# Hybrid encoder layer: output projection in token blocks, two of them projected ahead of FFN2's operands

## Chip, cores and metric

The kernel runs on one core of a Trainium2 chip. The metric is the device time of one execution in microseconds (us), as the median of several runs. TensorE is called PE here, VectorE DVE, ScalarE ACT, GpSimd POOL and SyncE SP, as in the profile.

## What is computed

One layer of an encoder on 1024 tokens of a new stream and 64 tokens of a running one, 1088 in all, with a model width of 1024 and FFN width of 2816. Cut to what matters here:

```python
def modulate(x, gain, shift, scale):
    return rms_norm(x, gain) * (1 + scale[:, None, :]) + shift[:, None, :]

def swiglu_ffn(h, w_up, w_down):
    gate, up = jnp.split(h @ w_up, 2, axis=-1)
    return (jax.nn.silu(gate) * up) @ w_down
...
    mixed = jnp.concatenate(
        [sb_o.reshape(B, T, SB_WIDTH).astype(x.dtype),
         jax.nn.silu(r_g) * head_group_norm(ret_o).reshape(B, T, RET_WIDTH).astype(x.dtype)],
        axis=-1) @ w_out
    x = x + g2[:, None, :] * mixed

    h = modulate(x, norm_ffn2, sh3, sc3)
    x = x + MACARON_WEIGHT * g3[:, None, :] * swiglu_ffn(h, ffn2_w_up, ffn2_w_down)
```

`sb_o` comes from stick-breaking attention, `ret_o` from a retention of four heads. Before this stands a first FFN of the same form.

## The kernel before

**Data.** Features lie on the partitions and tokens on the free axis. The residual stream is in eight tiles `A[0]` to `A[7]` of 128 x 1088. An fp32 product is made of three matmuls (`mm3`, L197 to L199): each operand is split into a high part, cast on ACT (L225 for data, L81 for weights), and a low part, subtracted on DVE or POOL (L226, L86); then high x high, low weight x high, and high weight x low are added in one PSUM bank. `H[k]` and `L[k]` hold the high and low part of an operand. Weights come in units of 1024 columns (`Units`): `load` starts the DMA of two halves of 128 x 512, `split` makes their two parts, `done` frees them. Tokens are cut into three chunks (384, 384, 320), or into four blocks of `BL` = 272.

**Output projection.** After the mix, `take` splits the eight concatenated head tiles into `H`, `L`. The last one (`lastk` = 7) is ready only when the last retention head is done. So `out_units` first adds up the seven `early` k for each of the eight output tiles d (one weight unit per d) and each chunk, 21 matmuls a group (tile `wo`), and is woven by estimated costs (`weave`) with the matmuls of that last head, `retain(3)`. The residual add (`resid`, L243) reads the bank and adds it to `A[d]`. Then a loop over the blocks 0, 2, 1, 3 makes the product with the last k alone, 3 matmuls for each d (tile `wl`), adds it to `A[d]`, stores `A[d]` for later (`xs`), and squares it for FFN2's norm (`Norm`): `square` on ACT with sums on POOL and DVE, `fold` on PE (tile `st`), `factors` on DVE and POOL (tile `rx`), and `rows` on PE (tile `rb`), which spreads the factors of a block over the partitions.

**FFN2's operands.** The up projection uses seven products instead of eight on 2 x 2 blocks (`ORDER`): the width is cut into k and k + 4, the tokens into blocks b and b + 2. Half s = 0 of each product takes blocks 0 and 2, half s = 1 blocks 1 and 3. For every k of 0 to 3 and every s, `x_build` multiplies four pieces of `A` by the norm's rows (L404, DVE), scales them on ACT (L407), forms t1 to t4 by differences (L412) and splits all seven operands (b11, t1, t2, b21, t3, t4, b22). In the kernel before, POOL takes the difference t3 and four of the seven splits, DVE the rest. The s = 0 builds are due at set times during the last two blocks of the output projection, the s = 1 builds beside up tile 0.

**Up tiles.** `Up.prep(f)` loads four weight halves of tile f, forms four sums (L466, DVE) and splits seven weights. `product(f, p, s)` is 12 matmuls of 272 columns, `read` takes the result from PSUM (L518, L521, L524, L528). A tile has 7 products x 2 halves x 12 = 168 matmuls. Tile 0 is written out by hand: the first three products by k as the operands come, for s = 0, and the same for s = 1; all others come product by product (`Up.tile`), with the conditioning's products beside tiles 1 to 18.

**What sets the order.** The program's order and the scheduler's own model set the order on each engine, and DVE keeps the program's order from tile 1 on. Each engine then works strictly through its own list.

## Time and profile before

| | |
|---|---|
| median of 3 runs | 2315.87 us (2313.78 to 2322.09) |
| the profiled execution | 2316.76 us, its span 2314.7 us |
| PE busy | 2184.9 us, 94% |
| DVE busy | 1505.9 us, 65% |
| POOL busy | 1051.6 us, 45% |
| ACT busy | 832.8 us, 36% |
| mean granted clock of PE | 0.971 |

Busy shares are means over the whole span. Two engines can each be far from full and yet bound a stage in turn, so the stage is read by windows and by waits. A matmul's listed duration is longer than the distance from one to the next, since they are pipelined; what a row of them costs is taken from their starts.

### The profile page before, as it was taken

Reading aid. Unit: us, or ns where it says so; the run is one execution under the profiler, and the core shown is the slowest. Engines: PE = TensorE matmul, PEld = TensorE weight load, DVE = VectorE, ACT = ScalarE, POOL = GpSimd, SP = SyncE. Lnnn points to the kernel's source line nnn. Section 1 sums busy time; section 2 is a strip of 40 time slices with the busy share of each in tenths; the row PEclk is TensorE's granted clock in tenths of the full one; section 3 lists DMA queues with packets and bytes.
Section 4 is the critical chain, followed back from the end, with each engine's and each line's share of the span. In section 5 each row is a group of like instructions: output and inputs, shape, how many; then the busy total and the mean of one; then the engine's idle time right before and its main releaser. Section 6 shows DMA issues by size and latency. Waiting matters only on the chain. (4 is left out here: it accounts for less than half of the span.)

```text
span 2314.7 us, 40167 instructions
## 1 busy us (share of the span) xinstructions
PE 2184.9 (94%) x15188; PEld 2140.0 (92%) x15188; DVE 1505.9 (65%) x2902; ACT 832.8 (36%) x1724; POOL 1051.6 (45%) x1004
## 2 busy tenths in 40 slices
PE   5899999999999988888989999968999999999999
PEld 4799999999999988888889998957999999999999
DVE  5767777755777878887773555386555555556666
ACT  5522322232221346655663333155332323322221
POOL 3444444453444565434443444266444444544442
PEclk8899999999999999999999999977999999999999
DMA  7233333336343321011001012122222222352322
GB/s 247 92 122 128 112 129 112 130 108 225 124 128 118 123 64 55 22 41 38 27 30 67 32 40 108 44 90 71 90 93 87 91 85 84 104 181 83 101 82 102
DMA packets 116609, 220.35 MB, mean 95 GB/s; under 512 B 14528, under 2 KB 55488, under 8 KB 116416
## 3 DMA queue, kind: packets, MB, share of 16 engines
q1 hardware_dynamic: 116416, 217.79, 27.9%
q8 instruction: 120, 1.97, 0.4%
q14 instruction: 73, 0.60, 0.1%
HBM read 174.88 MB, written 42.86 MB: 94 GB/s over the span
## 5 line engine op out<-in xcount | busy, mean ns | idle before, releaser
L243 DVE SCALAR_TENSOR_TENSOR A<-dn,mod,A 128x384 f32<-128x384 f32 (+1 forms) x704 | 329.6, 496 | 148.5 <-PE dn L199 147.6
L197 PE MATMUL dn<-hs,wh 128*128 128x384 f32 (+1 forms) x1056 | 348.7, 330 | 3.4 <-DVE A L243 3.4
L199 PE MATMUL dn<-hl,wh 128*128 128x384 f32 (+1 forms) x1056 | 348.1, 330 | 0.0
L198 PE MATMUL dn<-hs,wl 128*128 128x384 f32 (+1 forms) x1056 | 348.1, 330 | 0.0
L86 POOL TENSOR_TENSOR wl<-wr,wh 128x512 fp32r<-128x512 f32 x162 | 220.3, 1366 | 142.5 <-ACT wh L81 140.3
L197 PE MATMUL pj<-Hh,wh 128*128 128x384 f32 (+1 forms) x672 | 235.5, 350 | 1.7 <-DVE A L243 1.7
L226 POOL TENSOR_TENSOR hl<-hr,hs 128x384 fp32r<-128x384 f32 x132 | 131.3, 1011 | 228.9 <-ACT hs L225 227.0
L199 PE MATMUL pj<-Lh,wh 128*128 128x384 f32 (+1 forms) x672 | 222.9, 332 | 0.0
L198 PE MATMUL pj<-Hh,wl 128*128 128x384 f32 (+1 forms) x672 | 221.5, 330 | 0.0
L197 PEld LDWEIGHTS dn<-hs,wh 128*128 128x128 f32 x1056 | 199.1, 189 | 3.8 <-DVE A L243 3.7
L198 PEld LDWEIGHTS dn<-hs,wl 128*128 128x128 f32 x1056 | 199.1, 189 | 0.0
L199 PEld LDWEIGHTS dn<-hl,wh 128*128 128x128 f32 x1056 | 199.1, 189 | 0.0
L518 DVE TENSOR_TENSOR u<-p,p 128x272 f32<-128x272 f32 x176 | 77.3, 440 | 165.8 <-PE p L199 165.7
L225 ACT CAST hs<-hr 128x384 fp32r<-128x384 f32 x132 | 65.4, 496 | 323.2 <-PE dn L198 158.4
L197 PE MATMUL p<-xt,wh1s 128*128 128x272 f32 x528 | 154.2, 292 | 0.9 <-DVE u L518 0.9
L199 PE MATMUL p<-xt,wh1s 128*128 128x272 f32 x528 | 153.8, 291 | 0.7 <-DVE xt L226 0.7
L198 PE MATMUL p<-xt,wl1s 128*128 128x272 f32 x528 | 154.0, 292 | 0.0
L81 ACT CAST wh<-wr 128x512 fp32r<-128x512 f32 x162 | 98.1, 619 | 151.3 <-PE wo L199 50.8
L86 POOL TENSOR_TENSOR wl1a<-wr1a,wh1a 128x512 fp32r<-128x512 f32 x66 | 94.2, 1430 | 124.8 <-ACT wh1a L81 118.5
L86 POOL TENSOR_TENSOR wl2a<-wr2a,wh2a 128x512 fp32r<-128x512 f32 x66 | 87.5, 1326 | 102.1 <-ACT wh2a L81 102.0
L197 PEld LDWEIGHTS pj<-Hh,wh 128*128 128x128 f32 x672 | 127.9, 190 | 4.7 <-issue 2.7
L198 PEld LDWEIGHTS pj<-Hh,wl 128*128 128x128 f32 x672 | 128.0, 190 | 0.3
(324 smaller groups left out, 6685.6 us busy)
## 6 DMA issues: line engine op xcount, KB each, us to landing
wa<-in_wada SPq DMA_DIRECT2D x56, 512.0 KB, 3.6
hd<-hh SPq DMA_DIRECT2D x44, 544.0 KB, 2.7
wr1a<-in_wup SPq DMA_DIRECT2D x88, 256.0 KB, 2.8
wr<-in_wdn SPq DMA_DIRECT2D x88, 256.0 KB, 2.9
wr2a<-in_wup SPq DMA_DIRECT2D x88, 256.0 KB, 2.8
hr<-hd SPq DMA_DIRECT2D x88, 192.0 KB, 2.5
wr<-in_win SPq DMA_DIRECT2D x56, 256.0 KB, 2.7
au<-in_wada SPq DMA_DIRECT2D x16, 512.0 KB, 5.7
```

What stands on the lines that cost most here:

```text
L81: self.nc.scalar.copy(h, raw)
L86: self.nc.gpsimd.tensor_tensor(l, raw, h.bitcast(F32), op=ALU.subtract)
L197: nc.tensor.matmul(ps[:, :w], wh, xh, start=first, stop=False, skip_group_check=read_between)
L198: nc.tensor.matmul(ps[:, :w], wl, xh, start=False, stop=False, skip_group_check=read_between)
L199: nc.tensor.matmul(ps[:, :w], wh, xl, start=False, stop=last, skip_group_check=read_between)
L225: nc.scalar.copy(hi, src)
L226: eng.tensor_tensor(lo, src, hi.bitcast(F32), op=ALU.subtract)
L243: nc.vector.scalar_tensor_tensor(A[d][:, s0:s0 + sw], ps[:, s0 - c0:s0 - c0 + sw], mod[:, s, b, d:d + 1], A[d][:, s0:s0 + sw], op0=ALU.mul ...
L518: nc.vector.tensor_tensor(new(name), ps[:, :BL], v[y, s], op=ALU.add)
```

## The change

The output projection goes by blocks instead of chunks. Its early part makes blocks 0 and 2 alone, for d = 0 to 6, beside the last retention head; d = 7 and the product with the last k follow for these two blocks. Then blocks 1 and 3 are projected in full, 24 matmuls a group (tile `wb`), d in the order of `PAIRS`; for this the eight weight units are loaded and split a second time. Beside it FFN2's operands of s = 0 are built (`build_first`), all differences and splits on DVE now; b22 of s = 0 is split after the blocks are done. The residuals of `A[0]` and `A[4]` for blocks 1 and 3 go to separate tiles `xb`. Then come the norm of blocks 1 and 3 and the operands of s = 1, and up tiles 0 and 1 by pairs of blocks: s = 0 of tile 0, s = 0 of tile 1, s = 1 of tile 1, s = 1 of tile 0, the weights of tile 0 being loaded and split again for the last. Tiles 2 to 21 go as before, the conditioning's products beside 2 to 19.

```diff
+    PAIRS = [0, 4, 1, 5, 2, 6, 3, 7]
     wu.add([I["wout"][u] for u in range(9)])
+    wu.add([I["wout"][u] for u in PAIRS])
...
+    def x_first(pool):
+
+
+        keys = [(name, part, k, 0) for k in range(4) for name in SETS[:6] for part in range(2)]
+        for i in range(4):
+            put(pool.tile([P, NTOK], F32R, name=f"xe{i}", bufs=1), keys[4 * i:4 * i + 4])
+        places = [t[k][:, cols(blk)] for k in range(KT) for t in (H, L) for blk in (0, 2)]
+        X.update(zip(keys[16:], places))
+
+    def x_second():
+
+        keys = [(name, part, k, 1) for k in range(4) for name in SETS for part in range(2)]
+        places = [t[k][:, cols(blk)] for k in range(KT) for t in (H, L) for blk in (1, 3)]
+        X.update(zip(keys, places))
+        return keys[32:]
+
+    def over_x(kt, keys):
+        A[kt] = xpool.tile([P, NTOK], F32R, tag=f"A{kt}", name=f"x1A{kt}")
+        put(A[kt], keys)
...
-        less("t3", "b22", "b12", nc.vector if whole else nc.gpsimd)
+        less("t3", "b22", "b12", nc.vector)
...
-        for i, name in enumerate(SETS):
-            split_h(b[name], X[name, 0, k, s], X[name, 1, k, s], nc.gpsimd if i % 2 == 0 else nc.vector)
+    def x_split(b, names, k, s):
+        for name in names:
+            split_h(b[name], X[name, 0, k, s], X[name, 1, k, s], nc.vector)
...
-        def out_units(ds):
-            for d in ds:
+        def take(k, blk, eng):
+            split_h(A[k][:, cols(blk)], H[k][:, cols(blk)], L[k][:, cols(blk)], eng)
+
+        def out_units(blks):
+
+            for d in range(lastk):
                 u = U_WOUT + d
                 wu.load(min(u + 3, U_WOUT + 8))
-                for c in range(3):
-                    yield from out_early(d, c)
-                    if c == 1:
+                for i, blk in enumerate(blks):
+                    p = pt("pj", f"wo{d}_{blk}")
+                    for j, k in enumerate(early):
+                        acc_cols(p, u, [k], blk * BL, BL, j == 0, j == len(early) - 1)
+                        if j % 2 == 1:
+                            tick()
+                            yield 6 * BL / 2.4
+                    resid(p, BSEGS[blk], d, 5)
+                    yield 3 * BL / 2.4
+                    if i == 0:
                         wu.split(u + 1)
                 wu.done(u)
...
         hl_tiles("m", early)
-        for c in range(3):
+        for i, blk in enumerate((0, 2, 1, 3)):
             for k in early:
-                take(k, c)
+                take(k, blk, nc.gpsimd if (k + i) % 3 == 0 else nc.vector)
         for k in early:
             nc.sync.dma_start(A[k], xs[k])
-        weave(out_units(range(lastk)), retain(3), 7 * 63 * 155.0 * 0.8, RROOM)
+        weave(out_units((0, 2)), retain(3), 7 * 42 * 125.0 * 0.8, RROOM)
         hl_tiles("m", [lastk])
-        for c in range(3):
-            take(lastk, c)
+        for blk in (0, 2, 1, 3):
+            take(lastk, blk, nc.vector)
         nc.sync.dma_start(A[lastk], xs[lastk])
-        drain(out_units([lastk]))
...
+    xb = {d: hnpool.tile([P, 2 * BL], F32, name=f"xb{d}", bufs=1) for d in (0, 4)}
+
+    def xv(d, blk):
+        if d in xb and blk % 2 == 1:
+            return xb[d][:, blk // 2 * BL:(blk // 2 + 1) * BL]
+        return A[d][:, cols(blk)]
...
+    def build_first(k):
+
+        b = later[k] = x_parts([(name, kt, blk * BL, xv(kt, blk), ns[blk].rb[:, :BL]) for name, kt, blk in
+                                (("b11", k, 0), ("b12", k, 2), ("b21", k + 4, 0), ("b22", k + 4, 2))],
+                               hnpool, 2, k, 0, False, ("b22",))
+        x_split(b, SETS[:6], k, 0)
+
+    def finish_x(po, d, blk):
+        resid(po, BSEGS[blk], d, 5, xv(d, blk))
+        nc.sync.dma_start(xs[d][:, cols(blk)], xv(d, blk))
+        ns[blk].square(d, xv(d, blk))
...
-    for i, blk in enumerate((0, 2, 1, 3)):
-        c0 = blk * BL
-        for d in range(KT):
-            po = pt_any(f"wl{blk}_{d}", ("wt", "z"))
-            mm3(po, BL, *wu.get(U_WOUT + 8, d), H[lastk][:, c0:c0 + BL], L[lastk][:, c0:c0 + BL], True, True)
-            resid(po, BSEGS[blk], d, 5)
-            nc.sync.dma_start(xs[d][:, c0:c0 + BL], A[d][:, c0:c0 + BL])
-            ns[blk].square(d)
+    wu.load(U_WOUT + 9)
+    for blk in (0, 2):
+        for d in [lastk] + early:
+            po = pt_any(f"wl{blk}_{d}", ("wt", "z")) if d != lastk else pt("pj", f"wl{blk}_{d}")
+            if d == lastk:
+                acc_cols(po, U_WOUT + d, early, blk * BL, BL, True, False)
+            mm3(po, BL, *wu.get(U_WOUT + 8, d), H[lastk][:, cols(blk)], L[lastk][:, cols(blk)], d != lastk, True)
+            finish_x(po, d, blk)
             due(6 * BL / 2.4)
+            if d == 3 and blk == 0:
+                wu.split(U_WOUT + 9)
         at(now[0] + 2000, ns[blk].fold)
         at(now[0] + 2000, ns[blk].factors)
-        if i < 2:
-            at(now[0] + 4000, ns[blk].rows, "av" if blk < 2 else "ms")
-        if i == 1:
-            for k in range(4):
-                at(now[0] + 4100 + 1500 * k, x_build, k, 0, 2, rb_of, hnpool)
-        next(weights, None)
+        at(now[0] + 4000, ns[blk].rows, "av" if blk == 0 else "ms")
+    wu.done(U_WOUT + 7)
+    wu.done(U_WOUT + 8)
+    for k in range(4):
+        at(now[0] + 4100 + 6500 * k, build_first, k)
+    weights = up.prep(0)
+    for i, d in enumerate(PAIRS):
+        u = U_WOUT + 9 + i
+        if i < KT - 1:
+            wu.load(u + 1)
+        for blk in (1, 3):
+            po = pt("pj", f"wb{d}_{blk}")
+            ks = early + [lastk]
+            for j in range(0, KT, 2):
+                acc_cols(po, u, ks[j:j + 2], blk * BL, BL, j == 0, j == KT - 2)
+                due(6 * BL / 2.4)
+            finish_x(po, d, blk)
+            if blk == 1 and i < KT - 1:
+                wu.split(u + 1)
+        wu.done(u)
+        if i >= KT - 2:
+            next(weights)
     drain(weights)
-    wu.done(U_WOUT + 8)
     due(1e6)
+    for blk in (1, 3):
+        ns[blk].fold()
+        ns[blk].factors()
+        ns[blk].rows("av" if blk == 1 else "ms")
+    for i, d in enumerate((0, 4)):
+        over_x(d, [("b22", part, k, 0) for k in (2 * i, 2 * i + 1) for part in range(2)])
+    for k in range(4):
+        x_split(later[k], ("b22",), k, 0)
+    rest = x_second()
...
+    for k in range(4):
+        b = x_parts([(name, kt, blk * BL, xv(kt, blk), ns[blk].rb[:, :BL]) for name, kt, blk in
+                     (("b11", k, 1), ("b12", k, 3), ("b21", k + 4, 1), ("b22", k + 4, 3))],
+                    hnpool, 2, k, 1, False)
+        if k > 0:
+            over_x(k, rest[8 * k - 8:8 * k - 4])
+            over_x(k + 4, rest[8 * k - 4:8 * k])
+        x_split(b, SETS, k, 1)
+    hnpool.release()
+
+    prep = up.prep(1)
+    for p in ORDER:
+        up.product(0, p, 0)
+        up.read(0, p, 0)
+        next(prep, None)
+    drain(prep)
+    for p in ORDER:
+        up.product(1, p, 0)
+        up.read(1, p, 0)
+    prep = up.prep(0)
+    for k in range(4):
+            up.product(1, p, 1, [k])
+    for p in ORDER[:3]:
+        up.read(1, p, 1)
+        next(prep, None)
+    for p in ORDER[3:]:
+        up.product(1, p, 1)
+        up.read(1, p, 1)
+        next(prep, None)
+    drain(prep)
+    prep = up.prep(2)
+    for p in ORDER:
+        up.product(0, p, 1)
+        up.read(0, p, 1)
+        next(prep, None)
+    drain(prep)
...
```

What moves on DVE while the last two blocks are projected. Names: `wl`, `wb` are PSUM tiles of a group, `hn2b` and `hn2t` pieces and differences, `x0H`, `xe`, `Hm`, `Lm` operands; the source line numbers of the changed kernel are a few higher. Before, among the residuals of block 3:

```order
L412 TENSOR_TENSOR hn2t_17502<-hn2b_17493,hn2b_17490 128x272
L243 SCALAR_TENSOR_TENSOR A_7_6457<-wl_7_17524,mod,A_7_6457 128x272
L412 TENSOR_TENSOR hn2t_17504<-hn2b_17499,hn2t_17502 128x272
L226 TENSOR_TENSOR x0H_17223<-hn2t_17502,x0H_17223 128x272
L412 TENSOR_TENSOR hn2t_17508<-hn2b_17496,hn2t_17504 128x272
L226 TENSOR_TENSOR x0L_17224<-hn2b_17496,x0L_17224 128x272
L243 SCALAR_TENSOR_TENSOR A_0_6450<-wl_0_17545,mod,A_0_6450 128x208
L226 TENSOR_TENSOR x0H_17225<-hn2t_17508,x0H_17225 128x272
L243 SCALAR_TENSOR_TENSOR A_0_6450<-wl_0_17545,mod,A_0_6450 128x64
```

After the change, the residual of unit 4, block 3, and the next one:

```order
L246 SCALAR_TENSOR_TENSOR xb_17003<-wb_3_17390,mod,A_4_6454 128x208
L424 TENSOR_TENSOR hn2t_17429<-hn2b_17424,hn2t_17427 128x272
L424 TENSOR_TENSOR hn2t_17431<-hn2b_17424,hn2b_17418 128x272
L424 TENSOR_TENSOR hn2t_17433<-hn2b_17421,hn2t_17429 128x272
L229 TENSOR_TENSOR xe_17007<-hn2b_17415,xe_17007 128x272
L229 TENSOR_TENSOR xe_17007<-hn2t_17427,xe_17007 128x272
L229 TENSOR_TENSOR Hm_16282<-hn2t_17429,Hm_16282 128x272
L229 TENSOR_TENSOR Lm_16283<-hn2b_17421,Lm_16283 128x272
L229 TENSOR_TENSOR Hm_16284<-hn2t_17431,Hm_16284 128x272
L229 TENSOR_TENSOR Lm_16285<-hn2t_17433,Lm_16285 128x272
L246 SCALAR_TENSOR_TENSOR xb_17003<-wb_3_17390,mod,A_4_6454 128x64
L246 SCALAR_TENSOR_TENSOR A_1_6451<-wb_1_17456,mod,A_1_6451 128x272
```

Before, one or two building operations stand between residuals. Now three differences and six splits of one k stand between the two parts of one residual.

What moves on DVE in the building of s = 1. Before, from k = 1 (`x1A`, `xe` operands of k = 0, `rb_1`, `rb_3` the norm's rows):

```order
L404 TENSOR_TENSOR hn2b_17871<-A_1_6451,rb_1_17821 128x272
L226 TENSOR_TENSOR x1A_17856<-hn2b_17840,x1A_17856 128x272
L404 TENSOR_TENSOR hn2b_17874<-A_1_6451,rb_3_17825 128x272
L226 TENSOR_TENSOR xe_17775<-hn2t_17853,xe_17775 128x272
L404 TENSOR_TENSOR hn2b_17878<-A_5_6455,rb_1_17821 128x272
L404 TENSOR_TENSOR hn2b_17881<-A_5_6455,rb_3_17825 128x272
```

After the change, the same place for k = 1:

```order
L229 TENSOR_TENSOR Lm_16289<-hn2b_18066,Lm_16289 128x272
L229 TENSOR_TENSOR Hm_16290<-hn2t_18080,Hm_16290 128x272
L229 TENSOR_TENSOR Lm_16291<-hn2t_18082,Lm_16291 128x272
L229 TENSOR_TENSOR Hm_16292<-hn2b_18073,Hm_16292 128x272
L229 TENSOR_TENSOR Lm_16293<-hn2t_18084,Lm_16293 128x272
L229 TENSOR_TENSOR Hm_16294<-hn2t_18086,Hm_16294 128x272
L229 TENSOR_TENSOR Lm_16295<-hn2b_18076,Lm_16295 128x272
L416 TENSOR_TENSOR hn2b_18104<-A_2_6452,rb_1_17997 128x272
```

Before, DVE splits three of seven operands, between the next k's products; now it splits all seven in a row, and the next k's products come behind them.

What moves on PE between the halves of the first tiles. `p_20_0` is tile 0, s = 0, and `p_21_1` tile 1, s = 1. Before:

```order
L199 MATMUL p_20_0_17790<-x0H_17233,wh2s_0_17754 128x272
L197 MATMUL p_20_0_17790<-x0L_17236,wh2s_0_17754 128x272
L198 MATMUL p_20_0_17790<-x0L_17236,wl2s_0_17756 128x272
L199 MATMUL p_20_0_17790<-x0L_17236,wh2s_0_17754 128x272
L197 MATMUL p_20_1_18048<-x1A_17855,wh2a_0_17407 128x272
L198 MATMUL p_20_1_18048<-x1A_17855,wl2a_0_17409 128x272
```

After the change:

```order
L201 MATMUL p_21_1_18432<-x1A_18126,wl2a_1_18219 128x272
L200 MATMUL p_21_1_18436<-x1A_18127,wh2s_1_18238 128x272
L201 MATMUL p_21_1_18436<-x1A_18127,wl2s_1_18240 128x272
L200 MATMUL p_21_1_18440<-x1A_18127,wh2s_1_18242 128x272
L201 MATMUL p_21_1_18440<-x1A_18127,wl2s_1_18244 128x272
L202 MATMUL p_21_1_18432<-x1A_18126,wh2a_1_18217 128x272
L202 MATMUL p_21_1_18440<-x1A_18127,wh2s_1_18242 128x272
L202 MATMUL p_21_1_18436<-x1A_18127,wh2s_1_18238 128x272
L200 MATMUL p_21_0_18327<-xe_17005,wh2a_1_18282 128x272
L201 MATMUL p_21_0_18327<-xe_17005,wl2a_1_18284 128x272
L202 MATMUL p_21_0_18327<-xe_17005,wh2a_1_18282 128x272
```

Before, tile 0's half s = 1 follows the first three products of its half s = 0 and starts by k. Now the last by-k matmuls of tile 1's half s = 1, on operands of k = 3, stand ahead of four products of its half s = 0 (`p_21_0` on `xe`).

## Rows read from the trace of the kernel before

**Rows 1.** The page: busy tenths and granted clock in 40 slices of the span.
```profile
PE   5899999999999988888989999968999999999999
PEclk8899999999999999999999999977999999999999
```

**Rows 2.** Windows: length; busy PE, weight load, DVE, ACT, POOL; clock; DMA share, GB/s.
```profile
1409.08:1428.67 19.59, 14.55 (x76) 13.62 (x74) 14.56 (x26) 6.70 (x17) 10.39 (x9) 0.83 0.44 172
1428.67:1510.85 82.18, 82.18 (x514) 80.67 (x514) 30.68 (x89) 10.18 (x17) 22.90 (x24) 1.00 0.17 58
1510.85:1555.47 44.62, 23.61 (x147) 20.90 (x145) 39.56 (x82) 26.91 (x65) 30.47 (x37) 0.73 0.31 106
1555.47:1571.10 15.63, 15.29 (x87) 14.71 (x88) 11.63 (x29) 8.91 (x23) 5.68 (x7) 0.72 0.49 170
1571.10:1599.10 28.00, 16.82 (x76) 14.57 (x76) 23.41 (x43) 22.75 (x55) 19.94 (x21) 0.62 0.00 1
...
1624.20:1645.30 21.10, 21.10 (x170) 21.10 (x169) 11.70 (x20) 6.03 (x12) 10.64 (x8) 1.00 0.30 102
```

**Rows 3.** Waits of PE from 1409 to 1625: us in total, times, longest.
```profile
PE wl L197 <- DVE A L243: 11.8, 5, 3.8
```

**Rows 4.** Timeline of PE from 1414: start, us, instruction, idle before and releaser.
```profile
1414.14 0.38 PE L1206 MATMUL rsc<-qT,kT 128*128 128x128 f32 x2
...
1414.50 0.42 PE L197 MATMUL wo<-Hm,wh 128*128 128x384 f32 x1
...
1416.53 0.34 PE L199 MATMUL wo<-Lm,wh 128*128 128x384 f32 x1
1420.92 0.49 PE L1206 MATMUL rsc<-qT,kT 128*128 128x128 f32 x2 [4.05 <-DVE sm L1208]
```

**Rows 5.** Timeline of DVE from 1418.
```profile
1418.98 1.68 DVE L226 TENSOR_TENSOR Lm<-A,Hm 128x320 fp32r<-128x320 f32 x4
...
1422.58 0.62 DVE L243 SCALAR_TENSOR_TENSOR A<-wo,mod,A 128x384 f32<-128x384 f32 x1 [1.52 <-DMA A<-xs]
...
1427.17 0.41 DVE L1237 TENSOR_SCALAR yn<-ro,mv,ri 128x128 f32<-128x128 f32 x1 [0.72 <-POOL ri L1235]
```

**Rows 6.** Timeline of PE from 1555.
```profile
1555.47 0.56 PE L197 MATMUL p<-x0L,wh2s 128*128 128x272 f32 x1 [6.78 <-DVE A L243]
...
1557.39 0.43 PE L197 MATMUL p<-x0L,wh2a 128*128 128x272 f32 x1
1557.62 0.43 PE L198 MATMUL p<-x0L,wl2a 128*128 128x272 f32 x1
...
1565.47 0.91 PE L272 MATMUL st<-ones,sq 128*128 128x2 f32 x10
```

**Rows 7.** Groups on DVE, 1570 to 1594: count, busy us, mean ns, idle before.
```profile
L404 DVE TENSOR_TENSOR hn2b<-A,rb 128x272 f32<-128x272 f32 x12 | 4.9, 424 | 0.0
L226 DVE TENSOR_TENSOR x1A<-hn2t,x1A 128x272 fp32r<-128x272 f32 x4 | 4.0, 998 | 0.0
...
L412 DVE TENSOR_TENSOR hn2t<-hn2b,hn2b 128x272 f32<-128x272 f32 x4 | 1.7, 430 | 0.0
```

**Rows 8.** Groups on ACT, 1570 to 1594.
```profile
L407 ACT ACTIVATE hn2b<-hn2b,mod,scale_a 128x272 f32<-128x272 f32 x7 | 4.3, 612 | 1.7 <-DVE hn2b L404 1.4
```

**Rows 9.** The page: the costliest groups of instructions.
```profile
L86 POOL TENSOR_TENSOR wl<-wr,wh 128x512 fp32r<-128x512 f32 x162 | 220.3, 1366 | 142.5 <-ACT wh L81 140.3
```

**Rows 10.** Timeline of DVE, 1548 to 1590.
```profile
1548.14 6.29 DVE L226 TENSOR_TENSOR x0H<-hn2b,x0H 128x272 fp32r<-128x272 f32 x1
...
1571.18 1.37 DVE L412 TENSOR_TENSOR hn2t<-hn2b,hn2t 128x272 f32<-128x272 f32 x2 [0.26 <-ACT hn2b L407]
...
1589.25 1.36 DVE L412 TENSOR_TENSOR hn2t<-hn2b,hn2t 128x272 f32<-128x272 f32 x2 [0.82 <-ACT hn2b L407]
```

**Rows 11.** Timeline of POOL, 1549 to 1554.
```profile
1549.30 0.75 POOL L226 TENSOR_TENSOR x0L<-hn2b,x0L 128x272 fp32r<-128x272 f32 x1
...
1552.88 1.25 POOL L86 TENSOR_TENSOR wl2s<-wr2s,wh2s 128x512 fp32r<-128x512 f32 x1
```

162 lines of the change are left out of this document (52 added, 110 removed).

## Prediction

> **What bounds the kernel now.** I read the busy slices first, then the stretch they point at by windows, then TensorE's waits there, then single rows. In the slices [rows 1] the PE row is at 8 or 9 from the second slice on, but for one; that one and the next (slices 26 and 27 counted from 0, some 58 us each) have PE 6 and 8 and a granted clock of 0.7. They are the end of the output projection and the building of FFN2's operands. By windows [rows 2] PE has 82.18 of 82.18 us in the early output projection and 21.10 of 21.10 in a plain up tile, at clock 1.00. Between them it has 23.61 of 44.62 us in the last-k product and the first building, and 16.82 of 28.00 us in the second building. There DVE has 39.56 of 44.62 and 23.41 of 28.00. So this stretch ends by DVE, not by PE. The waits say the same: the last-k groups wait 11.8 us for the residual adds of L243 [rows 3]. The stretch that the change rewrites runs from the first output matmul at 1409.08 to the start of tile 2 at 1624.20, 215.1 us.
>
> **What PE must do in it.** A plain tile has 168 matmuls of 272 columns in 21.10 us [rows 2], so 0.1256 us each. After the change the projection has 4 blocks x 8 units x 8 k x 3 = 768 of them and two tiles 336, together 138.7 us. Retention stays: two score and two state matmuls set back the next output matmul from 1414.14 to 1414.50 [rows 4], and outputs and transposes come to somewhat more again, so I take 1 us for each of 9 chunks. A norm takes a fold of 0.91 us [rows 6] and about as much for its rows, 8 us for four blocks. This gives 157 us, 58 less than now: the most that the change can bring. What is left of it is decided by DVE, stage by stage.
>
> **Stage A: early product of blocks 0 and 2 beside retention.** Before, PE runs out of work at 1416.5 and gets the next matmul at 1420.92 after an idle 4.05 us, waiting for DVE [rows 4]: DVE works through the takes (the low halves of the operands) until 1420.6, and the first residual add waits until 1422.58 for the copy of A [rows 5]. After the change the takes hold the same columns, and only 2 x 21 matmuls lie before the first residuals instead of 3 x 21 larger ones, so PE runs dry at about 1416 again. In DVE's new order the residual of the first group follows the first normalised retention output. Statistics, the 0.72 us for POOL's power and 0.41 for the output [rows 5], then the add, make about 2.5 us behind 1422.6, so PE goes on at 1425.1. Then 252 matmuls are 31.7 us, eight chunks 8.2, the half clock after the idle costs 3.4 (now the first stretch has clock 0.83 [rows 2]: some 6.7 us at half), stalls 1.5: the end is at 1469.9.
>
> **Last unit and last k of blocks 0 and 2.** 90 matmuls are 11.3 us, folds and rows 2, and waits for residuals 2.5: now such groups wait 11.8 us in all four blocks [rows 3], most of it in the later two, which lie elsewhere now. This ends at 1485.7.
>
> **Stage B: blocks 1 and 3, beside the first building.** 16 groups of 24 matmuls are 48.2 us on PE, and one unit (two blocks) 6.03. DVE builds one k in 14 operations. One takes about 0.43 us alone [rows 7]; in a row they follow each other faster: four takes of 320 columns last 1.68 us [rows 5], 0.42 each, so 0.36 at 272 columns. Beside POOL one takes 0.998 (0.93 with the same overlap), while one with a PSUM operand (the products with the norm's rows) stays at 0.424 [rows 7]. So a k is 5.0 us, and the unit's residuals and sums add 1.6 or more: nearly 7 us against 6.03, four times over. On top come the splits of the repeated weights: 16 on POOL at 1.37 us each [rows 9]. Two of them stand in each unit, and each makes a DVE operation beside it 0.93 instead of 0.36, so over 1 us a unit. By the order there are two holds: the 64-column half of unit 4's residual stands behind nine building operations, and unit 2's residual behind all of k=3's. I take 3.7 and 2.8 us for them. With norms 2.2 and clock 1 the stage lasts 57.9 us, to 1543.6. For its bounds: no hold at all gives 51, and one DVE operation of 6.29 us, as the trace has it [rows 10], in each of two units gives 12.6 us of holds, 64 in all.
>
> The reloaded weights themselves cost nothing that ends last: 4 MB beside 48 us, where the DMA share of the neighbouring stages is 0.31 to 0.49 [rows 2]. POOL's 21.9 us lie beside PE. If that cover goes (a split that comes late), PE waits for a weight half, up to 1.4 us in a unit. The same holds for tile 0's weights, prepared a second time.
>
> **Stage C: second building beside tiles 0 and 1.** s=0 of both tiles is 168 matmuls, 21.1 us, and needs none of the new operands. The second building can begin when the rows of blocks 1 and 3 are there, about 6 us after the stage's start. It now lies on DVE alone: 16 products, 16 differences and 28 splits, with 6 tile reads, 4 weight sums and 2 factors between them, 72 operations. At 0.36 this is 25.9 us. ACT's scalings (0.612 us a whole block [rows 8], two of the four in two pieces) leave DVE waiting 0.82 us in each k now [rows 10], so 3.3. Seven weight splits on POOL beside it cost 0.57 each, 4.0. That is 33 us, 8.3 a k, where the k's now follow each other in 6.0 us (1571.18 to 1589.25 in three [rows 10]) because POOL takes a part. So the building ends 39 us after the stage's start. By PE's order four products of tile 1's first half stand behind its second half's by-k products, so about 180 of the 336 matmuls come after the building: 180 x 0.1256 = 22.6 us, and 2 us for the clock after the idle. The end is 64 us after the start, at 1607.6. Bounds: the building at today's 6.0 a k gives 54, and at 10.5 a k 73.
>
> **The sum.** 60.8 + 15.8 + 57.9 + 64 = 198.5 us instead of 215.1: 16.6 less. The later tiles, the down projection and the tail keep their order, and I cost them at 0: an up tile has PE full [rows 2]. The profiled execution took 2316.76 us (span 2314.7), 0.9 over the median of the runs, 2315.87; so I expect 2300 for the median too.
>
> **Rivals.** First, *DVE keeps up*: the holds of stage B vanish (-6.5) and stage C builds in 6.0 us a k (-9): 2300 - 16 = 2284. For it: in half of stage B's units POOL and DVE need not meet, and POOL has far less building work than now. Against it: 72 operations at 0.36 alone exceed 24 us.
>
> Second, *DVE is held by POOL's streaks*. While POOL ran seven operations without a gap (two of them in [rows 11]), one DVE split lasted 6.29 us and ended only with the streak [rows 10]. In the changed kernel weight splits come in pairs of 2.7 us. If DVE stands for the whole pair, that is 2.7 instead of the 1.1 I took: 4 pairs in stage B's building units +6.2, some 3.5 pairs in stage C +5.5. Together 2312, no difference. For it is that row; against it, the mean of 0.998 beside POOL [rows 7], which is an exchange of turns and not a full stop. The Trainium skill, "SBUF — State Buffer", section "Who interferes with whom", says that a DVE instruction with two SBUF inputs contends with a GpSimd one that reads SBUF, and that whoever has the shared ports blocks the other for its whole instruction. By that rule it would be this rival; the trace shows both pictures, the turns far more often.
>
> Third, on the other side: *the clock falls in stage B*. PE's granted clock is 1.00 where it never waits, 0.83 at 74% busy, 0.73 at 53% and 0.62 at 60% [rows 2]; at the low level a matmul of 272 columns follows after 0.23 us (1557.39 to 1557.62 [rows 6]). If the holds keep the clock at the low level through blocks 1 and 3, 384 matmuls take 87 us instead of the 56 that I have with holds: +31, 2331, slower. It decides when a wait in nearly every unit is as long as those of 1510 to 1555. Against it: at half clock PE has no waits, since DVE is then faster than it, and after the idle 6.78 us before 1555.47 [rows 6] the clock comes back by itself: the window from there to 1571.10, 98% busy, has 0.72 on average [rows 2]. The Trainium skill, "TensorE: Matmul & The Clock Gate", section "HAM oscillation — how this bites in real kernels", tells of a loop that waits in every pass and begins each at the low clock; it speaks for this rival, and no row here shows it over several passes.
>
> That the change doesn't do what it says is excluded by the order: the weights of units 0 to 7 stand there twice, and the first building lies between the groups of blocks 1 and 3.
>
> **How the numbers follow.** Chances: forecast 0.50, DVE keeps up 0.20, held by streaks 0.22, clock falls 0.08. The forecast's own bounds, stage B 51 to 64 and C 54 to 73, rarely fall at the same end; about half of each gives 2290 to 2309. The range 2282 to 2318 takes in the first two rivals, and leaves out the clock and what lies above all bounds. No change is within 0.5%, 11.6 us, which is about what a measurement of this kernel can tell. So faster needs less than 2304: 0.8 of the forecast, the first rival and little of the second, 0.63. Slower is the clock, 0.08, and the rest, 0.29, is no change.
>
> **What would show it.** Right: PE dry for over 8 us near 1416 to 1425; about 58 us from the first to the last group of blocks 1 and 3 at a clock of 0.9 or more; waits of these groups for residuals of 5 to 8 us in all; some 8 us from k to k in the second building, with PE idle over 10 us before tile 1's second half; tile 2 at about 1607. Wrong: a second building at 6 or at over 10 us a k; single DVE splits of more than 2 us beside POOL; a clock near 0.5 among blocks 1 and 3; waits of PE for weight halves; a changed duration after tile 2's start.

## The result, and the profile after

The changed kernel takes 2296.5 us (median of 4 runs, 2291.98 to 2298.47) beside 2318.98 us of the kernel before on the same chip: a ratio of 0.9896, 95% interval 0.9858 to 0.9934. Forecast were 2300 us in a range of 2282 to 2318, and faster with 0.63. A second comparison with more runs (below, the changed kernel again) gives 2295.46 against 2319.66, 0.9893, interval 0.9871 to 0.9915. So the kernel is faster by 22 to 24 us, where 16.6 were worked out.

The slices of the page after, against [rows 1]: the hole of 6 and 8 at clock 0.7 is gone.

```profile
PE   5899999999999988888999999998999999999999
PEclk9899999999999989999999999999999999999999
```

By windows, with the stages of the prediction as the cuts (columns as in [rows 2]): stage A, last unit and last k, stage B, the second building, from its end to tile 2, tile 2.

```profile
1416.10:1473.19 57.09, 50.98 (x378) 49.09 (x377) 34.23 (x99) 16.48 (x38) 29.71 (x32) 0.94 0.43 146
1473.19:1484.56 11.37, 11.37 (x96) 11.33 (x94) 7.17 (x18) 6.29 (x14) 7.42 (x8) 1.00 0.50 150
1484.56:1541.72 57.16, 53.37 (x419) 52.12 (x418) 41.73 (x101) 35.17 (x81) 34.77 (x30) 1.00 0.41 125
1541.72:1578.09 36.37, 29.90 (x194) 27.33 (x192) 28.65 (x77) 26.77 (x66) 12.62 (x12) 0.86 0.11 34
1578.09:1605.96 27.87, 24.09 (x181) 22.92 (x181) 14.94 (x27) 10.73 (x21) 16.79 (x13) 1.00 0.43 148
1605.96:1627.06 21.10, 21.10 (x170) 21.10 (x169) 12.17 (x20) 6.98 (x14) 12.86 (x9) 1.00 0.29 96
```

From the first output matmul (1416.10) to tile 2 (1605.96) it is 189.9 us now, and was 215.1: 25.2 less. From tile 2 to the last matmul's start both have 687. The profiled execution is only 18.3 us shorter than before (2298.47 against 2316.76) because this stretch began 7.0 us later, behind a part of the program in which PE's order is the same in both kernels; the last section shows how far this start varies. What PE waited for in the stretch, against the 11.8 us of [rows 3]:

```profile
PE p L200 <- DVE u L521: 5.7, 6, 2.2
PE rsc L1210 <- DVE sm L1212: 4.8, 1, 4.8
PE p L200 <- ACT g L537: 2.8, 1, 2.8
PE wb L200 <- DVE A L246: 2.1, 2, 1.1
PE wb L200 <- DVE xb L246: 1.0, 1, 1.0
```

PE is not busy for 20.1 of the 189.9 us, where it was 37.5 of 215.1; and the granted clock, which lies at 0.62 to 0.83 in four windows of [rows 2], is nowhere under 0.86 in these.

### The profile page after: what moved, and what is told of

Its sections match the earlier page's. It is cut to its first block, busy times and chain, and to the rows that moved or that the text cites. A ratio compares the mean times of both kernels' runs of the same rounds, so it can differ in the third digit from the quotient of the medians.

```text
span 2296.7 us, 40613 instructions
## 1 busy us (share of the span) xinstructions
PE 2184.1 (95%) x15356; PEld 2140.8 (93%) x15356; DVE 1503.6 (65%) x2934; ACT 844.5 (37%) x1755; POOL 1051.9 (46%) x989
## 4 chain that ended last, share of the span: by engine, by line
PE 80%; DVE 8%; POOL 4%; issue 4%; ACT 3%; DMA 1%; SPq 0%; POOLq 0%; DVEq 0%; ACTq 0%
PE p L201 13%; PE p L200 13%; PE p L202 13%; PE dn L200 8%; PE dn L201 7%; PE dn L202 7%; PE pj L200 3%; PE pj L202 3%; PE pj L201 3%; DVE f L961 2%; DVE s L964 1%; ACT f L953 1%; PE av L1006 1%; POOL rh L218 1%; PE wt L995 1%
## 5 line engine op out<-in xcount | busy, mean ns | idle before, releaser
L86 POOL TENSOR_TENSOR wl<-wr,wh 128x512 fp32r<-128x512 f32 x178 | 242.9, 1373 | 143.2 <-ACT wh L81 140.0
L81 ACT CAST wh<-wr 128x512 fp32r<-128x512 f32 x178 | 107.7, 619 | 133.3 <-PE dn L202 39.5
```

The lines of the kernel that those rows point to most:

```text
L81: self.nc.scalar.copy(h, raw)
L86: self.nc.gpsimd.tensor_tensor(l, raw, h.bitcast(F32), op=ALU.subtract)
```

## The experiments

The stretches are named as in the prediction: A from the first output matmul to the last unit's first, L from there to the first of blocks 1 and 3, B to their last, C from there to tile 2. Each run has one profile; of the program ahead and behind nothing differs but when A begins, so a part's worth is read from its stretch. All times in us; the ratio is to the kernel before on the same chip.

| run | A | L | B | C | sum | median | ratio, interval |
|---|---|---|---|---|---|---|---|
| changed kernel | 57.1 | 11.4 | 57.2 | 64.2 | 189.9 | 2296.5 | 0.9896, 0.9858 to 0.9934 |
| the same again | 57.3 | 11.4 | 57.2 | 64.5 | 190.3 | 2295.46 | 0.9893, 0.9871 to 0.9915 |
| POOL's share in s = 1 | 57.1 | 11.4 | 57.2 | 68.9 | 194.5 | 2300.19 | 0.9920, 0.9891 to 0.9949 |
| building due later | 56.5 | 11.4 | 60.5 | 64.3 | 192.6 | 2296.13 | 0.9896, 0.9869 to 0.9924 |
| rows made late | 56.9 | 11.4 | 56.3 | 85.4 | 210.0 | 2313.14 | 0.9966, 0.9950 to 0.9982 |
| one tile by halves | 57.2 | 11.4 | 57.2 | 60.8 | 186.5 | 2290.92 | 0.9875, 0.9849 to 0.9900 |
| the same, POOL's share | 57.2 | 11.4 | 58.2 | 64.3 | 191.1 | 2294.81 | 0.9897, 0.9872 to 0.9922 |
| takes spread | 58.0 | 11.4 | 57.2 | 63.9 | 190.5 | 2297.36 | 0.9909, 0.9879 to 0.9938 |
| own buffer for a12 | 57.1 | 11.4 | 59.9 | 63.4 | 191.9 | 2299.79 | 0.9918, 0.9889 to 0.9947 |
| splits doubled | 57.2 | 11.4 | 75.7 | 63.9 | 208.2 | 2311.23 | 0.9967, 0.9950 to 0.9985 |
| one tile, takes, norm | 52.6 | 11.4 | 59.9 | 61.4 | 185.4 | 2290.98 | 0.9873, 0.9851 to 0.9895 |
| one tile, takes | 52.2 | 11.4 | 58.7 | 60.8 | 183.0 | 2291.67 | 0.9881, 0.9860 to 0.9902 |
| the same, weights earlier | 51.4 | 11.4 | 57.5 | 66.1 | 186.4 | 2291.64 | 0.9878, 0.9858 to 0.9897 |

A stage's length also holds the clock that PE was granted in that one execution. B of the changed kernel, and B of the version with one tile and all takes on DVE, have the same waits of PE (2.1 and 1.0 us for residuals, 0.7 for a fold):

```profile
1484.56:1541.72 57.16, 53.37 (x419) 52.12 (x418) 41.73 (x101) 35.17 (x81) 34.77 (x30) 1.00 0.41 125
```

```profile
1481.42:1540.13 58.71, 54.92 (x420) 53.68 (x419) 41.72 (x101) 35.17 (x81) 34.77 (x30) 0.97 0.38 122
```

The 1.55 us between them are PE busy for longer at 0.97 instead of 1.00. So a difference of under 2 us between two profiles' stages is put down to an edit only where a wait shows it.

My theory was that the gain is the cover of the first building by blocks 1 and 3, and that what is left is DVE's second building. The rivals were that the pairs of tiles bring the gain, and that weights or POOL bound the rest.

**Is it the cover?** The first attempt only made the building due later in the program:

```diff
-        at(now[0] + 4100 + 6500 * k, build_first, k)
+        at(5e5 + 10 * k, build_first, k)
```

> One part undone: the building of s = 0 is due only after the last group of blocks 1 and 3, and not beside them. Theory (that the building lies beside the projection is what the change brings): four k's of about 5 to 7 us each come onto the path, less the 3.1 us of holds that they now cause among blocks 1 and 3: 18 to 25 us longer, total 2315 to 2322, the time of the kernel before. Rival (the gain comes from the pairs of blocks in tiles 0 and 1 and from the shorter early part): at most 8 us longer, total up to 2305.

It answered nothing. The first products with the norm's rows still start among blocks 1 and 3 (1481.59, where that stage runs from 1477.65 to 1538.1): the scheduler took what was ready, whatever the program's due time. (B is 3.3 us longer, 2.9 of it PE busy at a clock of 0.94.) So the rows themselves were put behind the last group, in banks that the groups hold until then:

```diff
-        at(now[0] + 4000, ns[blk].rows, "av" if blk == 0 else "ms")
+        at(4e5, ns[blk].rows, "pj")
...
-        at(now[0] + 4100 + 6500 * k, build_first, k)
+        at(5e5 + 10 * k, build_first, k)
```

> The cover taken away for good: the norm's rows of blocks 0 and 2 are made in the PSUM banks of the output groups, after the last of them, so that no building of s = 0 can start beside blocks 1 and 3 (making it due later in the program did not move it). Theory (that the building lies beside the projection is what the change brings): four k's of 14 DVE operations, 5.0 us and 1.3 us of ACT's scalings each, 25 us, come behind the projection, which gets 3 to 4 us shorter without holds and rows: stretch from first output matmul to tile 2 from 189.9 to 208 to 214 us, total 2315 to 2322, the time of the kernel before. Rival (products of s = 0 then lie beside the second building and hide most of it): at most 10 us longer, total up to 2307.

The sum grew by 20.1 us to 210.0, all of it in C, and the median went to 2313.14 (2320.07 for the kernel before on that chip); the sum is in the theory's range, the total 2 us under it. Windows of this run: B, a part of B, and C:

```profile
1483.58:1539.92 56.34, 53.58 (x408) 53.33 (x407) 20.63 (x41) 18.61 (x37) 30.45 (x30) 0.94 0.41 127
1493.00:1503.00 10.00, 10.00 (x63) 10.00 (x63) 1.13 (x3) 2.47 (x5) 3.19 (x4) 0.74 0.25 81
1539.92:1625.34 85.42, 64.10 (x386) 59.49 (x385) 65.43 (x164) 56.19 (x131) 29.86 (x24) 0.76 0.21 67
```

and C of the changed kernel:

```profile
1541.72:1605.96 64.24, 53.99 (x375) 50.24 (x373) 43.59 (x103) 37.50 (x86) 29.40 (x24) 0.92 0.25 83
```

The theory holds: undoing this one part takes away 20 of the 25 us. C is 21.2 us longer; PE is without work for 11.1 of these, and for 10.1 it is busy longer with nearly the same matmuls, at a granted clock of 0.76 instead of 0.92. So the cover saves clock as well as waiting. What the building costs B can't be read from B's 56.3 us, 0.9 less than with it, since here PE waited 2.8 us for a fold,

```profile
PE st L275 <- DVE sq L268: 2.8, 1, 2.8
```

and had a clock of 0.74 in the 10 us behind that. By the waits of the changed kernel the building costs B 3.1 us of residuals, for 21 us of DVE's work that lies beside PE (41.73 against 20.63). What the other parts of the change bring no run separates.

**Do the pairs of tiles pay?** Tile 1 in full after tile 0, and tile 0's weights prepared once:

```diff
-    prep = up.prep(1)
     for p in ORDER:
         up.product(0, p, 0)
         up.read(0, p, 0)
-        next(prep, None)
-    drain(prep)
-    for p in ORDER:
-        up.product(1, p, 0)
-        up.read(1, p, 0)
-    prep = up.prep(0)
+    prep = up.prep(1)
     for k in range(4):
         for p in ORDER[:3]:
-            up.product(1, p, 1, [k])
+            up.product(0, p, 1, [k])
     for p in ORDER[:3]:
-        up.read(1, p, 1)
+        up.read(0, p, 1)
         next(prep, None)
     for p in ORDER[3:]:
-        up.product(1, p, 1)
-        up.read(1, p, 1)
-        next(prep, None)
-    drain(prep)
-    prep = up.prep(2)
-    for p in ORDER:
         up.product(0, p, 1)
         up.read(0, p, 1)
...
```

(The conditioning's products lie beside tiles 1 to 18 again.)

> One part undone: only tile 0 goes by halves (s = 0, then s = 1 by k as the operands come); tile 1 follows in full, and the weights of tile 0 are prepared once. Theory (half of tile 1 covers part of the second building): 84 matmuls, 10.6 us, lose their place beside the building, less what the second preparation of tile 0's weights costs (DVE waits 2.0 to 2.6 us at a time for weight halves and buffers, some 4 us of the 27.9 from the building's end to tile 2): 6 to 10 us longer, total 2303 to 2307. Rival (the second preparation eats the cover): within 3 us of the changed kernel.

C became 3.4 us shorter, not 6 to 10 longer: theory and rival both missed, on the same side. Its windows are B, the second building, and from its end to tile 2:

```profile
1482.02:1539.17 57.15, 53.38 (x420) 52.13 (x419) 41.69 (x101) 35.17 (x81) 34.74 (x30) 1.00 0.40 125
1539.17:1572.39 33.22, 25.10 (x162) 23.06 (x161) 26.54 (x75) 24.16 (x60) 4.89 (x7) 0.81 0.19 60
1572.39:1599.95 27.56, 27.52 (x214) 27.30 (x214) 15.57 (x29) 10.83 (x21) 15.53 (x12) 0.98 0.30 98
```

The clock does not explain it: C has 0.89 here, 0.92 in the changed kernel. In the pairs' version the building's window is 36.37 us with 12.62 us of POOL, here 33.22 with 4.89. And behind the building the pairs leave PE 3.8 us without work (24.09 of 27.87) where one tile fills it (27.52 of 27.56). Where the pairs lose it shows on DVE, in the changed kernel's second building: the products with the norm's rows begin each k.

```profile
1545.88 0.44 DVE L416 TENSOR_TENSOR hn2b<-xb,rb 128x272 f32<-128x272 f32 x1 [1.69 <-PE rb L224]
...
1554.76 1.47 DVE L416 TENSOR_TENSOR hn2b<-A,rb 128x272 f32<-128x272 f32 x4
...
1561.58 1.47 DVE L416 TENSOR_TENSOR hn2b<-A,rb 128x272 f32<-128x272 f32 x4
...
1566.88 0.69 DVE L469 TENSOR_TENSOR wr2s<-wr2a,wr2s 128x512 f32<-128x512 f32 x1 [2.55 <-DMA wr2a<-in_wup]
...
1571.01 1.47 DVE L416 TENSOR_TENSOR hn2b<-A,rb 128x272 f32<-128x272 f32 x4
...
1577.66 0.43 DVE L229 TENSOR_TENSOR x1A<-hn2b,x1A 128x272 fp32r<-128x272 f32 x1
```

The k that lasts 9.4 us has a sum of tile 1's weights in it that waits 2.55 us for a load, with the building queued behind it on DVE.

**Is it that load?** The fourth weight half got its own buffer and went out with the other three:

```diff
-            self.load(f, "a12")
+            if not self.own:
+                self.load(f, "a12")
             self.split(f, "s3")
```

(`own`, set ahead of `up.prep(0)`, adds a12 to the first loads, in a buffer of its own pool.)

> One wait taken away: in FFN2 the fourth weight half of a tile (a12) gets a buffer of its own and is loaded together with the other three, instead of waiting for one of the four shared buffers. Theory (beside the second building DVE is held by the preparation of weights, that is, its last sum waits 2.55 us for a late load, then 2.2 us twice): these waits go, the stretch from blocks 1 and 3 to tile 2 shrinks from 64.2 to 60 to 62 us. Rival (the sum only waits where another wait, for POOL's low halves or ACT's scalings, ends next): 63.5 to 64.5 us, no change.

The rival came true: C is 63.4, 0.8 less. B is 2.7 longer, at a clock of 1.00, with PE's waits for residuals at 5.3 us instead of 3.1. DVE's waits for weights from 1475 to 1606, in the changed kernel:

```profile
DVE wr2s L469 <- DMA wr2a<-in_wup: 7.9, 3, 3.1
...
DVE wr2a L469 <- POOL wl2a L86: 4.7, 2, 2.6
```

and in this run:

```profile
DVE wr2a L476 <- POOL wl2a L86: 4.7, 3, 2.6
...
DVE wr2s L476 <- POOL wl2s L86: 3.7, 3, 1.4
```

The last sums no longer wait 7.9 us for the load but 3.7 for POOL's low halves; the first sums wait as long as before. So the wait for the load was one of several that end close together, and taking it alone gives little.

**Would POOL's share help?** t3 and four of seven splits of s = 1 back on POOL:

```diff
-            split_h(b[name], X[name, 0, k, s], X[name, 1, k, s], nc.vector)
+            split_h(b[name], X[name, 0, k, s], X[name, 1, k, s],
+                    nc.gpsimd if s == 1 and SETS.index(name) % 2 == 0 else nc.vector)
```

(and `less("t3", ...)` on `nc.gpsimd` for s = 1.)

> One part undone: in the building of s = 1 the difference t3 and four of the seven splits of each k go to POOL again, as in the kernel before; the building of s = 0 stays on DVE. Theory (the second building ends by DVE's 60 operations): the products of the four k's now start 6.8, 9.4 and 7.1 us after one another; with POOL's share they come at about 6.0, the building takes 26 us instead of 32.2, and the stretch from the last matmul of blocks 1 and 3 to tile 2 shrinks from 64.1 to 57 to 60 us; total about 2291. Rival (that stretch ends by the weights of tiles 0 and 1, whose low halves are made on POOL): POOL's weight splits stand behind building splits, waits for weight halves grow, the stretch stays at 64 or grows to 68; total 2297 to 2301.

The stretch grew to 68.9, as the rival said in number, but not by its reason: PE waits for no weight half. Its longest wait is for a read of PSUM, which stands on DVE behind the building:

```profile
PE p L200 <- DVE c L522: 9.8, 1, 9.8
```

So PE did 158 matmuls up to the building's end instead of 194, and the rest came behind it:

```profile
1533.70:1569.86 36.16, 22.85 (x158) 21.65 (x156) 30.09 (x54) 25.32 (x61) 25.50 (x29) 0.83 0.10 34
```

The building took as long as without POOL, 32.0 us on DVE (1537.85 to 1569.86) against 32.2, though DVE had 20 operations less: those left became slower. Groups on DVE of this run over the building:

```profile
L424 DVE TENSOR_TENSOR hn2t<-hn2b,hn2t 128x272 f32<-128x272 f32 x8 | 6.4, 803 | 1.1 <-ACT hn2b L419 1.0
L416 DVE TENSOR_TENSOR hn2b<-A,rb 128x272 f32<-128x272 f32 x12 | 4.7, 425 | 0.0
```

and of the changed kernel:

```profile
L424 DVE TENSOR_TENSOR hn2t<-hn2b,hn2t 128x272 f32<-128x272 f32 x8 | 3.5, 435 | 0.5 <-ACT hn2b L419 0.5
```

The same eight differences take 803 ns instead of 435; the products with a PSUM operand stay at 425. To have this without weight splits beside it, the same share was given to POOL in the version with one tile:

> Tile 0 alone by halves, as in the run with one tile, and the second building shared with POOL again (t3 and four of seven splits). There no weight split lies beside the building. Theory (DVE and POOL only exchange turns: two engines do these operations no faster than DVE alone, as in the run with POOL's share, where the building took 32.0 us against 32.2): the building stays at 28.5 to 30 us (29.0 with one tile), total 2289 to 2293. Rival (POOL's share helps where no weight split stands beside it, as in the kernel before with 6.0 us a k): 26 us, the stretch from blocks 1 and 3 to tile 2 from 60.8 to 58, total 2288.

Its edit is the two lines above on top of the one-tile edit. The building lasts 30.2 us (1539.48 to 1569.7) against 29.1, and C 64.3 against 60.8. So in these two orders POOL's help in the second building is worth nothing, or less. Whether it would help in the first, beside B, was not tried.

**How much may POOL do beside B?** Each reloaded unit split twice:

```diff
+        raws = wu.raw.get(u + 1)
...
                 wu.split(u + 1)
+                for x, (h, l) in enumerate(wu.parts[u + 1]):
+                    h2 = wu.high(raws[x], f"d{u}_{x}")
+                    wu.low(raws[x], h2, f"d{u}_{x}")
```

> One cost doubled: each reloaded weight unit of blocks 1 and 3 is split twice (two casts on ACT and two differences on POOL more in a unit, 14 of each in all; their results are not used). Theory (a POOL split costs a DVE operation beside it one turn, about 0.57 us): the holds of PE among blocks 1 and 3, 3.1 us now, grow to 4 to 5 us, that stage from 57.2 to 58 to 59.5 us, the rest unchanged. Rival (DVE stands still for a whole streak of POOL, now of four splits, 5.5 us): single DVE operations of over 2 us, holds of 9 us or more, the stage 63 us or more.

B grew by 18.5 us to 75.7, beyond both: 11.9 us in which PE is without work, and 6.6 busy for longer at a clock of 0.91. But the rival's own sign is missing: no single DVE operation lasts over 1.53 us. ACT is the engine that stands, as its waits in B say:

```profile
ACT whd L81 <- POOL wld L86: 10.9, 5, 4.3
...
ACT wh L81 <- POOL wld L86: 3.4, 2, 2.7
```

The extra parts take buffers from the seven that all weight parts of a kind share, so ACT's next cast waits until POOL has used one up, and the building's scalings and casts stand behind it on ACT: DVE then waits 4.9 us for scalings and PE up to 5.4 us for one residual. The run doubled a buffer's use along with the splits, so it does not price a split alone. It shows that the cover in B has an end: the cast of a weight that waits for POOL holds everything behind it on ACT.

**PE's first idle.** The takes of blocks 1 and 3 spread over the early units and given to POOL, with A copied back by blocks:

```diff
+                    if d > 0:
+                        for k in early[i::2]:
+                            if k % 6 == d - 1:
+                                for b in (1, 3):
+                                    take(k, b, nc.gpsimd)
+                                    nc.sync.dma_start(A[k][:, cols(b)], xs[k][:, cols(b)])
...
-        for i, blk in enumerate((0, 2, 1, 3)):
+        for i, blk in enumerate((0, 2)):
...
```

> A part added: the takes of blocks 1 and 3 come after those of blocks 0 and 2, spread over the early output units and all on POOL, and the copy of A comes back by blocks, so that the first residual adds need only blocks 0 and 2. By the order 9 takes instead of 12 stand ahead of the first retention product on DVE. Theory (PE's idle 4.8 us at the start, and the half clock of 6.7 us behind it, come from DVE's takes): 3 takes of 0.93 us less, idle under 2.5 us, the stretch from the first output matmul to the last unit's 57.1 us shrinks by 3 to 6 us. Rival (the copies of A and the chain of retention set that start): the idle moves to the first residual add or to retention's outputs behind POOL's takes, and the stretch changes by less than 1.5 us either way.

The rival held, A is 58.0: the wait for the first retention product fell from 4.8 to 1.2 us, and a wait for retention's output, whose power stands behind takes and weight splits on POOL, rose from 0.5 to 5.5:

```profile
PE ytp L1247 <- DVE yn L1241: 6.0, 2, 5.5
PE rsc L1210 <- DVE sm L1212: 1.2, 1, 1.2
```

What the runs with POOL's share showed suggested the opposite: all takes on DVE.

```diff
-                take(k, blk, nc.gpsimd if (k + i) % 3 == 0 else nc.vector)
+                take(k, blk, nc.vector)
```

Together with one tile by halves, and with the norm of block 1 put beside the last group of block 3, this is

> A version from what the runs showed: tile 0 alone by halves, all 28 takes on DVE alone, and the fold, factors and rows of block 1 already beside the last group of block 3. Theory (an operation on POOL costs DVE beside it more than it takes over): 28 takes at 0.35 are 9.9 us and end about 2 us earlier than now with 9 or 10 on POOL, so PE's idle 4.8 us at the start becomes 2 to 3.5 and the stretch to the last unit's first matmul 57.2 us becomes 53 to 55.5; the second building starts about 3 us earlier after blocks 1 and 3, and the stretch from there to tile 2 becomes 57 to 59 us instead of 60.8. Together from 186.5 to 180 to 184, total about 2286. Rival for the takes (DVE has more to do and PE waits longer): idle 6 us or more, that stretch 58 to 60. Rival for the norm (the building is held by ACT's scalings and by block 3's rows in any case): 60 to 61 us, unchanged.

The takes did what was expected: A fell to 52.6, and PE's wait at the start to 2.4 us. The norm did not: the building's first product came 3 us earlier after B, but block 3's rows ended only 0.4 us earlier, and B grew by 2.7, in part by a clock of 0.97. So it was taken out again:

> What held of the versions before: tile 0 alone by halves, and all takes on DVE; the norm of block 1 again behind the last group. Theory (the two act in stretches of their own and add up): stretches of 52.6, 11.4, 57.2 and 60.8 us, from first output matmul to tile 2 181 to 183 us instead of 190 of the changed kernel; total 2284 to 2288. Rival (what the takes gain is given back where the last blocks' groups wait for DVE): the stage of blocks 1 and 3 grows to 59 us or more, 184 to 187 in all, total 2290.

52.2, 11.4, 58.7 and 60.8: the sum is 183.0. B grew as the rival said, but not for its reason: PE's waits for DVE there are those of the changed kernel, and the 1.5 us are the clock's, as shown ahead of the experiments. Of the 4.9 us that A is shorter than in the changed kernel, 3.2 are PE's idle time and 1.7 a clock of 0.97 instead of 0.94. The takes on DVE in this run, and below them those of the changed kernel that lie beside POOL's:

```profile
1417.14 8.64 DVE L229 TENSOR_TENSOR Lm<-A,Hm 128x272 fp32r<-128x272 f32 x24
```

```profile
1417.66 4.61 DVE L229 TENSOR_TENSOR Lm<-A,Hm 128x272 fp32r<-128x272 f32 x5
```

0.36 us each alone, 0.92 each beside POOL. Weights prepared two units earlier were tried on top:

```diff
-        if i >= KT - 2:
-            next(weights)
+        if i >= KT - 4:
+            next(weights, None)
```

> The same, and the preparation of tile 0's weights begins two units earlier among blocks 1 and 3, so that fewer of its POOL splits (1.27 to 1.28 us each) stand just ahead of the norm's power for blocks 1 and 3 on POOL. Theory (the second building starts late because of these splits): its first products come 1 to 1.5 us earlier, total 1 us less than without. Rival (two splits still stand there, or the earlier casts and sums hold the residuals): within 1 us, or the stage of blocks 1 and 3 longer by 1 to 3 us.

B is shorter by 1.2, by a clock of 1.00 instead of 0.97, and C longer by 5.3. C without and with the edit:

```profile
1540.13:1600.92 60.79, 51.17 (x374) 48.79 (x373) 42.24 (x102) 35.10 (x81) 20.54 (x18) 0.92 0.23 78
```

```profile
1534.87:1601.02 66.15, 56.43 (x374) 54.17 (x373) 42.13 (x106) 36.20 (x84) 22.80 (x19) 0.82 0.25 83
```

PE is without work as long as before (9.7 against 9.6 us) and does the same 374 matmuls in 5.3 us more, at a clock of 0.82 instead of 0.92. The building's first product also came 7.0 us after B, not 4.2: against the theory, later. Whether the late start brought the low clock or the clock the late start, this run does not show.

The changed kernel itself ran once more beside these:

> The changed kernel as it is, on the same chip as the version with takes and norm: stretches of 57.1, 11.4, 57.2 and 64.2 us again, each within 0.5 us, whatever the time at which the first output matmul starts; total 2292 to 2299, some 10 us above the other.

Its stretches came again within 0.3 us, though the first began at 1417.93. By the sums, one tile with all takes on DVE is 7 us shorter than the changed kernel; the medians, 2291.67 and 2295.46, lie that way but their ranges overlap (2286.57 to 2295.59 and 2290.3 to 2300.32, on different chips), so the total does not yet show it. It beats the kernel before clearly.

## Why the prediction was right, step by step

- **Bound and direction: right.** The stretch ended by DVE's building, covering one of the two buildings was most of the gain (the run with rows made late), and the rest of the program kept its time.
- **Stage A, 60.8 forecast, 57.1 measured.** The step that failed is "so PE goes on at 1425.1", with the costs of half clock and retention added behind it. PE did run dry, and the residual of the first group did stand where the order put it (16.8 us after the start, 16.0 forecast). But PE came back earlier, after 10.2 us, for retention and the rest of the second group:

```profile
1421.22 0.29 PE L202 MATMUL wo<-Lm,wh 128*128 128x272 f32 x1
1426.28 0.80 PE L1210 MATMUL rsc<-qT,kT 128*128 128x128 f32 x2 [4.77 <-DVE sm L1212]
...
1432.91 0.90 DVE L246 SCALAR_TENSOR_TENSOR A<-wo,mod,A 128x272 f32<-128x272 f32 x2
```

  The half clock (6.7 us from 1426.28 to 1433) fell on this work, which was done before the residual came. Half clock, retention and the wait for the residual lay beside one another; I had put them in a row.
- **Last unit and last k, 15.8 forecast, 11.4 measured.** The terms "waits for residuals 2.5" and "folds and rows 2" were mis-sized: PE was busy 11.37 of 11.37 us. The residuals of two blocks, with no building beside them, never hold PE; of the folds and rows only one fold lies here, and three of the 16 groups fell into the next stage with the rest.
- **Stage B, 57.9 forecast, 57.2 measured.** The holds stood at the two places named, the residuals of unit 4 (1.03 us before 1506.13) and unit 2 (1.14 before 1522.47), and at one more (0.94), but sum to 3.1 us, not 6.5: weight splits seldom met the building, and most DVE operations took their 0.43. Part of this was made up for: a fold, two sets of rows and the three last groups of block 2 took some 4 us here, where the sum has "norms 2.2", and PE waited 0.7 for the fold.
- **Stage C, 64.0 forecast, 64.2 measured, partly by luck.** The building began 4.2 us after the stage's start (6 forecast) and took 32.2 us for 33. But contention with POOL, 4.0 in the sum, is nearly absent (the differences have 435 ns), and DVE's waits are others: 3.5 us for the norm's rows, half of it ahead of the building, and 2.55 for a load. From its end to tile 2 it took 27.9 us, 24.6 forecast: PE waits there for reads of PSUM that stand on DVE behind the sums of tile 0's second preparation. These sums wait themselves:

```profile
1581.95 1.42 DVE L469 TENSOR_TENSOR wr2a<-wr2a,wr2a 128x512 f32<-128x512 f32 x2 [2.07 <-POOL wl2a L86]
...
1591.84 0.69 DVE L469 TENSOR_TENSOR wr2s<-wr2a,wr2s 128x512 f32<-128x512 f32 x1 [2.21 <-DMA wr2a<-in_wup]
```

  That reloaded weights "cost nothing that ends last" is thus wrong for this preparation. With one tile the wait for the load in the building and the second preparation both go, and C is 60.8.
- **The sum** came out 8.6 us too long, 3.7 in A and 4.4 in the last unit. (The least work of PE adds up to 155.7 us, not 157, but no term hangs on it.)
- **That 2296.5 lies only 3.5 us from 2300 is in part luck.** The stretch gained 25.2 us for 16.6, but the kernel before has a median of 2318.98 here, 3.1 more than the forecast set out from, and the changed kernel's two profiles came to the stretch 7 and 9 us later than the one of the kernel before.
- **The first rival, DVE keeps up,** is 12.5 us under the measured time. It was right that operations would seldom meet POOL, and wrong in what it took from that: the building went by 8 us a k (6.8 to 9.4), not 6.0.
- **The signs.** Of the right ones, B's length and clock and the 8 us from k to k came; PE was dry for 4.8 us at the start, not over 8, waits for residuals in B were 3.1, not 5 to 8, and tile 2 came at 1606 only because the start was 7 us late. Of the wrong ones, PE waited for a weight half once, for 1.0 us.
- **Streaks on POOL: not here.** The longest DVE operation in the stretch that one row holds alone is 1.57 us. The Trainium skill, "SBUF — State Buffer", section "Who interferes with whom", says that a DVE instruction with two SBUF inputs contends with a GpSimd one that reads SBUF, and that one with at most one SBUF input, outside the two-port modes, does not; the trace agrees (two SBUF operands: 0.92 beside POOL, 0.36 alone; a PSUM operand: 0.425 either way). A stop over several POOL operations, as [rows 10] once had it, came in the stretch of no run here; a port held for one POOL operation would be a turn, not such a stop, so the prediction's step from the one to the other does not follow.
- **The clock in B** was 1.00 with three waits of about 1 us. But it is less safe than that: with the same waits it was 0.97 in two runs (one tile and takes, with and without the norm), and it was 0.94 with the building due later (waits up to 2.0 us) and with the rows made late (one of 2.8). It cost 1.5 us without the norm and 2.9 with the building due later, and the clock came back. The third rival's price, 31 us from a clock that stays low through the stage, came in none, and with holds up to 5.4 us (splits doubled) the stage's clock was 0.91.

## What to carry to other kernels

When two engines share operations whose operands both lie in SBUF, measure one engine alone first: here such an operation of the takes took 0.92 us on DVE beside POOL instead of 0.36, giving work back to POOL made neither second building shorter, and taking work from POOL made the takes shorter. Put work that bounds a stage beside a stage in which another engine is the bound, and see in the trace that the scheduler's place is the one meant, since a later due time in the program did not move the building out of the stage. Before work of a later tile is pulled in as cover, count what it brings along on the engine that is the bound: half of tile 1 gave 84 matmuls of cover, and its weight sums, with tile 0's weights prepared twice, cost more than that. And compare the granted clock of a stage before a difference of 1 or 2 us is put down to an edit.

## What the runs showed of the hardware that was not expected

The time at which the first output matmul starts differs from 1408.1 to 1417.9 us between the profiled executions, though PE's order up to there is the same in all. Windows of 400 us in the attention, from the run with POOL's share (start at 1408.08) and from the changed kernel again (1417.93):

```profile
800.00:1200.00 400.00, 352.93 (x2249) 331.62 (x2248) 317.50 (x536) 241.77 (x514) 193.78 (x251) 0.96 0.12 41
```

```profile
800.00:1200.00 400.00, 354.30 (x2191) 333.28 (x2191) 311.52 (x525) 234.44 (x496) 189.52 (x247) 0.93 0.12 41
```

In the same time the later one has done 58 matmuls less, some 10 us at this pace, at a granted clock of 0.93 instead of 0.96. The kernel before (start at 1409.08) has 0.96 there, the first profile of the changed kernel (1416.10) 0.93. PE is busy 88% of this time, and the clock of such a stretch differs from run to run by as much as a part of this change is worth; that is why the parts were compared by their own stretches. What decides it no run shows. B is the same on a small scale: equal waits, and a clock of 1.00 in one execution and 0.97 in another.
